# Attention scores: the rotary keys' high part times the queries' low part as 64-row matmuls, two key tiles side by side, four key tiles in one group

## The chip, the core and the metric

The kernel runs on one core of one Trainium2 chip. The metric is the time of one execution on the device in microseconds (us); the time before is the median of three runs, 1285.17 us (1284.21 to 1286.22).

The names of the engines: PE is TensorE (matmuls; PEld are its weight loads), DVE is VectorE, ACT is ScalarE, POOL is GpSimd, SP is SyncE, which issues most DMAs here.

## The reference

One layer of a bidirectional encoder, 2048 tokens of width 1024, all in float32. A combined projection feeds a gated linear attention (group A) and a latent attention with softmax (group B); their outputs pass one output projection, and a LayerNorm closes the layer. The change is in group B alone:

```python
def mla_branch(c_q, c_kv, k_rope, gate, positions, q_norm_g, w_uq, kv_norm_g, w_ukv):
    q = (rms_norm(c_q, q_norm_g) @ w_uq).reshape(B, S, MLA_HEADS, MLA_D_NOPE + MLA_D_ROPE)
    kv = (rms_norm(c_kv, kv_norm_g) @ w_ukv).reshape(B, S, MLA_HEADS, MLA_D_NOPE + MLA_DV)
    q_nope = q[..., :MLA_D_NOPE] * scale
    q_rope = apply_rope(q[..., MLA_D_NOPE:], positions) * scale
    k_nope, v = kv[..., :MLA_D_NOPE], kv[..., MLA_D_NOPE:]
    k_r = apply_rope(k_rope, positions)
    ...
        s = (jnp.einsum('bqhd,bkhd->bhqk', qn, k_nope, preferred_element_type=jnp.float32)
             + jnp.einsum('bqhr,bkr->bhqk', qr, k_r, preferred_element_type=jnp.float32))
        p = jax.nn.softmax(s, axis=-1)
        return jnp.einsum('bhqk,bkhv->bqhv', p.astype(v.dtype), v)
```

There are 4 heads; the plain part of a key has 128 numbers, the rotary part 64, and the rotary key is shared by all heads.

## The kernel before

**Precision.** A float32 operand that TensorE is to multiply is split into a high part (rounded to the type that TensorE takes in one pass, `F32R`) and a low part, the rest. A product of two such operands is made as three matmuls: high x high, high x low, low x high. `hi` makes a high part on ACT, `lo` a low part on DVE or POOL.

**Stages.** `sweep_a` (the linear attention's products), `late_gates`, `sweep_c` (the latent projections and the linear attention's end), then `attention`, whose tail is the output projection.

**Attention.** There are 16 blocks, one for each pair of a head and 512 queries. The key side is absorbed into the queries, so a block multiplies its queries with the 16 tiles of 128 latent keys that all heads share. A block goes through them in 8 steps j of two key tiles each. `scores(i, j)` fills one of two PSUM buffers `pS` (two banks each, one bank for each key tile e) with five matmuls of 128x512 for each key tile: latent keys' high part times the queries' high and low part, their low part times the high part, and two for the rotary part. For those the tile `kr` (profile name `krs`) holds a key's 64 rotary numbers twice over its 128 rows: high part on rows 0 to 63, low part on rows 64 to 127. The queries' parts `rh` and `rl` are fetched twice, on both halves of the rows; so `kr` x `rh` gives (high + low) x high in one matmul, and `kr` x `rl` gives (high + low) x low.

The other operations of a step, in the order of their dependencies:

- `copy(i, j)` on ACT (L1578) copies the scores from PSUM to SBUF; `smax(i, j)` on DVE (L1591, "max") takes the running maximum, reading the same PSUM buffer. The buffer is free for `scores(i, j+2)` after both.
- After step 7, `tmax`, `rmax` and `bmax` turn the maxima into one value for each query, on all rows.
- `sub` (DVE), `exp` (ACT, L1619), `phi` ("hi", ACT, L371, high part) and `plo` ("lo", POOL, L377, low part) make the softmax's numerators, and `pv(i, j)` multiplies them with the latent values: six matmuls (L425 to L427) that sum into `o`.
- `acc` and `tot` sum the numerators, `tsum` (four transposes on PE, L1678) and `rcp` make the reciprocal.
- After the last `pv`, `oh` (ACT, tile `ofh`) and `ol` (DVE, tile `ofl`) split `o`, `y` (three matmuls) multiplies it with the value weights, `yc` copies and stores.

**The order is written out by hand.** Each operation is put into a list with a place, counted in steps: `scores(i, j)` stands at 8i + j, an operation n of the same step at 8i + j + PLACE[n][j], and those that come once for each block at 8i + 7 + PLACE[n]. The list is sorted by place, and the operations are issued in that order; `in_order` ties each instruction to the one before it on its own engine, so every engine executes its part of the list in the order of the places and waits where an input isn't ready.

An operation of block i therefore runs while later blocks' scores are made. Around the change, in step 2 to 4 of block i, the places give these orders:

```
PE:  scores(i,2)  pv(i-2,6)  pv(i-2,7) at 2.45  scores(i,3)  tsum(i-2)  scores(i,4)  pv(i-1,0)
ACT: copy(i,2)  acc0  exp(i-1,1)  oh(i-2) at 3.34  hi(i-1,1) at 3.41  copy(i,3) at 3.73  hi(i-1,2)
DVE: max(i,2)  sub(i-1,4)  sub(i-1,5)  ol(i-2)  max(i,3)
```

Of the kernel before, what the change touches and what calls it, by code (L numbers as in the profile page):

```python
# [9 lines left out]
F32 = mybir.dt.float32  # L10
# [8 lines left out]
P = 128  # L19
# [10 lines left out]
QB = 512  # L30
# [51 lines left out]
    exp=(10.18, 9.95, 7.63, 9.15, 8.26, 9.12, 7.84, 8.01),  # L82
    hi=(10.39, 10.41, 9.81, 10.32, 9.82, 10.74, 10.53, 10.47),
    lo=(11.99, 11.22, 11.21, 12.62, 11.98, 11.51, 10.87, 10.63),
    pv=(12.35, 12.1, 11.89, 12.65, 12.27, 12.25, 12.14, 11.45),
    acc=(12.45, 11.78, 12.32, 0, 10.57, 11.24, 10.03, 9.22),
    acc0=10.78,
    tmax=1.26,
# [18 lines left out]
    pv=(16.29, 16.53, 21.45, 24.62, 26.22, 30.32, 41.89, 43.83),  # L107
# [17 lines left out]
    whole=(24.99, 55.73),  # L125
# [235 lines left out]
class K:  # L361
# [981 lines left out]

    def c_krsh(self, d):
        d["krs"] = self.w1.tile([P, 2, 64], F32R, tag="krs", name=f"krs{d['c']}")
        self.hi(d["krs"][:, 0], d["kr"][:, 0])

    def c_krsl(self, d):
        self.lo(d["krs"][:, 1], d["kr"][:, 0], d["krs"][:, 0], "pool")

    def c_vh(self, d):
        self.hi(self.vh[:, d["c"]], d["ckv"])
# [181 lines left out]
    def attention(self):  # L1534
        tc, nc = self.tc, self.nc
        mm = nc.tensor.matmul
        V, G, Ac = nc.vector, nc.gpsimd, nc.scalar
        NP = NKT // 2
        with ExitStack() as ctx:
# [5 lines left out]
            pM, pO, pX, pA, pS = bank("pM"), bank("pO"), bank("pX"), bank("pA"), bank("pS", 2)  # L1545
            blocks = [(h, b) for b in range(NQB) for h in range(H)]
            nb = len(blocks)
            stt = [dict(s=[None] * NP) for _ in blocks]

            def fetch(i):  # L1550
# [5 lines left out]
                for p, src in zip("hl", self.qr_s[b]):  # L1556
                    q.append(qp.tile([P, QB], F32R, tag="wz", name=f"r{p}{i}"))
                    for r in (slice(0, 64), slice(64, 128)):
                        nc.sync.dma_start(q[-1][r].bitcast(F32), src[h])

            def scores(i, j):


                d = stt[i]
                qh, ql, rh, rl = d["q"]
                ps = d["ps", j] = pS.tile([P, 2, QB], F32, tag="pS", name=f"pS{i}_{j}")
                for e in range(2):
                    kh, kl, kr = (t[:, 2 * j + e] for t in (self.ckvT_h, self.ckvT_l, self.kr))
                    mm(ps[:, e], kh, qh, start=True, stop=False)  # L1569
                    mm(ps[:, e], kh, ql, start=False, stop=False)  # L1570
                    mm(ps[:, e], kl, qh, start=False, stop=False)  # L1571
                    mm(ps[:, e], kr, rh, start=False, stop=False)  # L1572
                    mm(ps[:, e], kr, rl, start=False, stop=True)  # L1573

            def copy(i, j):
                d = stt[i]
# [166 lines left out]
            def put(place, fn, *a):  # L1743
                todo.append((place, len(todo), fn, a))

            def at(f, i, j=None):
                p = PLACE_LAST.get(f, PLACE[f]) if i == nb - 1 else PLACE[f]
                return p[j] if isinstance(p, tuple) else p
# [3 lines left out]
            for i in range(nb):  # L1752
                for j in range(NP):
                    t = NP * i + j
                    put(t, scores, i, j)
                    for n, f in (("copy", copy), ("max", smax), ("sub", sub), ("exp", exp), ("hi", phi), ("lo", plo),
                                 ("pv", pv), ("acc", acc)):
                        if n != "acc" or j != SUM_POOL[0] or i == nb - 1:
                            put(t + at(n, i, j), f, i, j)
                put(NP * i + at("acc0", i), acc0, i)  # L1760
                for n, f in (("tmax", tmax), ("rmax", rmax), ("bmax", bmax)) + {nb - 1: (), nb - 2: own_late}.get(i, own):
                    put(NP * i + NP - 1 + at(n, i), f, i)
                if i + 2 < nb:
                    put(NP * i + 4.05, fetch, i + 2)
# [298 lines left out]
```

## Time and profile before

| | |
|---|---|
| median of three runs | 1285.17 us (1284.21 to 1286.22) |
| the profiled execution's own time | 1286.1 us |
| its span, first to last instruction | 1284.3 us |
| mean granted TensorE clock | 0.998 |
| PE busy in the span | 98% |
| DVE, ACT, POOL busy in the span | 70%, 59%, 59% |

The attention's matmuls of scores run from 598 to 1079 us of the span. In the profile, a line such as `PE L1573 MATMUL pS<-rl,krs 128*128 128x512` is a matmul on 128 rows and 128 columns of the array with 512 columns streamed through it; "busy, mean ns" is its duration, which overlaps with the next matmul's. In a timeline the first number is the start and the second the duration (for "xN", from the first start to the last end), and in square brackets stands the idle time of the engine just before, with what ended it. In the table of windows each engine has its busy time and its number of instructions.

### The profile page before, as it was taken

How to read it: one execution, taken by the hardware profiler on the slowest of the kernel's cores; microseconds unless marked ns; L12 is line 12 of the kernel's file. 1: busy time of each engine (PE TensorE's matmuls, PEld its weight loads, DVE VectorE, ACT ScalarE, POOL GpSimd, SP SyncE). 2: the span in 40 equal slices, each digit the busy share in tenths (PEclk: the TensorE clock that was granted, in tenths of full speed). 3: DMA queues.
4: the chain of work that ended last, by engine and by line, in shares of the span. 5: the costliest groups of instructions: out<-in, count | busy, mean ns of one | idle time of the engine just before them, and what ended most of it. 6: DMA issues, size and time to landing. Idle time of an engine off the chain costs nothing.

```text
span 1284.3 us, 19837 instructions
## 1 busy us (share of the span) xinstructions
PE 1259.7 (98%) x7050; PEld 1109.9 (86%) x7050; DVE 899.4 (70%) x1602; ACT 755.5 (59%) x1230; POOL 761.1 (59%) x476
## 2 busy tenths in 40 slices
PE   7999999999999999999999999999999999999997
PEld 7999999999889999999788888888888888887886
DVE  6635554544575555554888888888888888479997
ACT  7544343444565655555788888888888888511110
POOL 0132323222367666650498888889999999944541
PEclk9999999999999999999999999999999999999999
DMA  8223444444755666547201111111133110375752
GB/s 293 78 79 108 115 111 114 115 105 126 255 171 184 205 205 210 194 149 228 76 1 42 41 42 50 46 54 58 58 89 93 41 42 9 123 227 193 220 189 99
DMA packets 135746, 155.25 MB, mean 121 GB/s; under 512 B 43510, under 2 KB 86142, under 8 KB 135648
## 3 DMA queue, kind: packets, MB, share of 16 engines
q1 hardware_dynamic: 127584, 151.86, 38.4%
q0 software_dynamic: 672, 2.10, 0.4%
q8 instruction: 56, 0.92, 0.4%
q10 hardware_dynamic: 7392, 0.03, 0.3%
q14 instruction: 42, 0.34, 0.2%
HBM read 100.43 MB, written 53.51 MB: 120 GB/s over the span
## 4 chain that ended last, share of the span: by engine, by line
PE 82%; DMA 5%; DVE 4%; ACT 2%; issue 2%; POOL 2%; SPq 2%; DVEq 0%; POOLq 0%; ACTq 0%
PE pz L1237 6%; PE ipm L1308 5%; PE o L425 4%; PE o L426 4%; PE o L427 4%; PE pS L1569 4%; PE pS L1570 4%; PE pS L1572 4%; PE pS L1571 4%; PE pS L1573 4%; PE ipa L425 4%; PE ipa L427 4%; PE ipa L426 4%; PE ipg L427 2%; PE ipg L425 2%
## 5 line engine op out<-in xcount | busy, mean ns | idle before, releaser
L377 POOL TENSOR_TENSOR pl<-s,ph 128x1024 fp32r<-128x1024 f32 x128 | 306.4, 2411 | 57.7 <-ACT ph L371 53.8
L1591 DVE TENSOR_TENSOR rm<-pS,rm 128x512 f32<-128x512 f32 x210 | 144.8, 689 | 36.7 <-ACT s L1578 31.5
L1578 ACT ACTIVATE s<-pS 128x1024 f32<-128x1024 f32 x128 | 131.2, 1026 | 61.8 <-PE pS L1573 52.0
L1615 DVE TENSOR_TENSOR s<-s,mb 128x1024 f32<-128x1024 f32 x128 | 151.2, 1212 | 8.9 <-PE mb L1609 8.2
L371 ACT ACTIVATE ph<-s 128x1024 fp32r<-128x1024 f32 x128 | 135.1, 1057 | 16.9 <-PE o L427 16.4
L1619 ACT ACTIVATE s<-s 128x1024 f32<-128x1024 f32 x128 | 131.4, 1050 | 12.2 <-DVE s L1615 12.1
L425 PE MATMUL ipa<-wah,xah 128*128 128x384 f32 (+1 forms) x384 | 129.7, 338 | 5.5 <-ACT wah L371 5.5
L426 PE MATMUL ipa<-wal,xah 128*128 128x384 f32 (+1 forms) x384 | 124.5, 324 | 0.5 <-DVE wal L377 0.5
L427 PE MATMUL ipa<-wah,xal 128*128 128x384 f32 (+1 forms) x384 | 124.4, 324 | 0.0
L1569 PE MATMUL pS<-qh,ckvT_h 128*128 128x512 f32 x256 | 102.7, 401 | 2.0 <-ACT s L1578 1.2
L1072 POOL TENSOR_TENSOR Sb<-Sb,Us 64x512 f32<-64x512 f32 x15 | 20.9, 1394 | 136.9 <-DVE Us L1064 127.8
L425 PE MATMUL o<-ph,vh 128*128 128x512 f32 x256 | 101.0, 395 | 0.0
L1570 PE MATMUL pS<-ql,ckvT_h 128*128 128x512 f32 x256 | 100.0, 391 | 0.0
L1572 PE MATMUL pS<-rh,krs 128*128 128x512 f32 x256 | 99.9, 390 | 0.0
L1571 PE MATMUL pS<-qh,ckvT_l 128*128 128x512 f32 x256 | 99.9, 390 | 0.0
L1573 PE MATMUL pS<-rl,krs 128*128 128x512 f32 x256 | 99.8, 390 | 0.0
L427 PE MATMUL o<-ph,vl 128*128 128x512 f32 x256 | 99.7, 389 | 0.0
L426 PE MATMUL o<-pl,vh 128*128 128x512 f32 x256 | 99.6, 389 | 0.0
L1642 DVE TENSOR_TENSOR ap<-ap,s 128x512 f32<-128x512 f32 x120 | 83.1, 693 | 2.7 <-ACT s L1619 0.7
L377 POOL TENSOR_TENSOR xal<-xaf,xah 128x1024 fp32r<-128x1024 f32 x12 | 29.7, 2477 | 87.8 <-ACT xah L371 87.8
L377 POOL TENSOR_TENSOR ol<-of,oh 128x512 fp32r<-128x512 f32 x32 | 43.2, 1352 | 62.6 <-ACT oh L371 61.9
L425 PEld LDWEIGHTS ipa<-wah,xah 128*128 128x128 f32 x384 | 72.9, 190 | 7.8 <-ACT wah L371 5.5
(308 smaller groups left out, 3595.6 us busy)
## 6 DMA issues: line engine op xcount, KB each, us to landing
xcf<-xT_dram SPq DMA_DIRECT2D x16, 512.0 KB, 5.1
xr<-x_dram SPq DMA_DIRECT2D x16, 512.0 KB, 6.4
out_dram<-rr SPq DMA_DIRECT2D x32, 256.0 KB, 2.2
xaf<-xT_dram SPq DMA_DIRECT2D x14, 512.0 KB, 4.2
oib<-oi_s SPq DMA_DIRECT2D x16, 256.0 KB, 4.0
qdb<-qd_s SPq DMA_DIRECT2D x16, 256.0 KB, 4.0
SU<-su_s SPq DMA_DIRECT2D x16, 256.0 KB, 4.1
ub<-u_s SPq DMA_DIRECT2D x16, 256.0 KB, 4.2
```

Source lines behind the costliest of these rows:

```text
L371: return nc.scalar.activation(dst, src, AF.Copy).ins
L377: return e.tensor_tensor(dst, src, hi.bitcast(F32), ALU.subtract).ins
L425: mm(out, ah, bh, start=start, stop=False)
L426: mm(out, ah, bl, start=False, stop=False)
L427: mm(out, al, bh, start=False, stop=stop)
L1569: mm(ps[:, e], kh, qh, start=True, stop=False)
L1570: mm(ps[:, e], kh, ql, start=False, stop=False)
L1571: mm(ps[:, e], kl, qh, start=False, stop=False)
L1572: mm(ps[:, e], kr, rh, start=False, stop=False)
L1573: mm(ps[:, e], kr, rl, start=False, stop=True)
L1591: V.tensor_tensor(d["rm"], src[:, e], d["rm"], ALU.max)
L1615: V.tensor_tensor(s, s, d["mb"][:, None, :].to_broadcast([P, 2, QB]), ALU.subtract)
```

## The change

The halves of `kr` are laid out the other way round for odd key tiles: low part on rows 0 to 63, high part on rows 64 to 127. So of two neighbouring key tiles the even one has its high part on the upper half of the rows and the odd one on the lower half.

In blocks 1 to 15, `scores` leaves out the matmul `kr` x `rl`. In its place a new operation `halves(i, j)`, for even j at place j + 0.22, makes only high part x `rl`, as matmuls of 64 rows: for the two key tiles of step j (one on rows 0 to 63, one on rows 64 to 127), and then for the two of step j + 1. The first two close the sums of step j; the last two open the buffer of step j + 1, to which `scores(i, j + 1)` then adds. The product of the keys' low part and the queries' low part is left out there. Block 0 keeps the five matmuls. `pv(i, 7)` gets another place, 12.3 instead of 11.45: in step 3 of block i + 2, behind `scores` and `tsum` and just ahead of `oh`.

```diff
-    pv=(12.35, 12.1, 11.89, 12.65, 12.27, 12.25, 12.14, 11.45),
+    pv=(12.35, 12.1, 11.89, 12.65, 12.27, 12.25, 12.14, 12.3),
...
     def c_krsh(self, d):
         d["krs"] = self.w1.tile([P, 2, 64], F32R, tag="krs", name=f"krs{d['c']}")
-        self.hi(d["krs"][:, 0], d["kr"][:, 0])
+        self.hi(d["krs"][:, d["j"]], d["kr"][:, 0])
 
     def c_krsl(self, d):
-        self.lo(d["krs"][:, 1], d["kr"][:, 0], d["krs"][:, 0], "pool")
+        j = d["j"]
+        self.lo(d["krs"][:, 1 - j], d["kr"][:, 0], d["krs"][:, j], "pool")
...
+            def bank_pair(i, j):
+                if ("ps", j) not in stt[i]:
+                    stt[i]["ps", j] = pS.tile([P, 2, QB], F32, tag="pS", name=f"pS{i}_{j}")
+                return stt[i]["ps", j]
+
             def scores(i, j):
-                d = stt[i]
-                qh, ql, rh, rl = d["q"]
-                ps = d["ps", j] = pS.tile([P, 2, QB], F32, tag="pS", name=f"pS{i}_{j}")
+                qh, ql, rh, rl = stt[i]["q"]
+                begun = i > 0 and j % 2
+                whole = i == 0
+                ps = bank_pair(i, j)
                 for e in range(2):
                     kh, kl, kr = (t[:, 2 * j + e] for t in (self.ckvT_h, self.ckvT_l, self.kr))
-                    mm(ps[:, e], kh, qh, start=True, stop=False)
+                    mm(ps[:, e], kh, qh, start=not begun, stop=False)
                     mm(ps[:, e], kh, ql, start=False, stop=False)
                     mm(ps[:, e], kl, qh, start=False, stop=False)
-                    mm(ps[:, e], kr, rh, start=False, stop=False)
-                    mm(ps[:, e], kr, rl, start=False, stop=True)
+                    mm(ps[:, e], kr, rh, start=False, stop=bool(begun))
+                    if whole:
+                        mm(ps[:, e], kr, rl, start=False, stop=True)
+
+            def halves(i, j):
+
+                rl = stt[i]["q"][3]
+                for n in (j, j + 1):
+                    ps = bank_pair(i, n)
+                    for e in range(2):
+                        r = slice(64 * e, 64 * e + 64)
+                        mm(ps[:, e], self.kr[r, 2 * n + e], rl[r], start=n > j, stop=n == j)
...
                     put(t, scores, i, j)
+                    if i and j % 2 == 0:
+                        put(t + 0.22, halves, i, j)
```

## The prediction

> **What bounds the kernel now.** I read the page first: engine shares, then the group of the product that is changed.
>
> ```profile
> span 1284.3 us, 19837 instructions
> PE 1259.7 (98%) x7050; PEld 1109.9 (86%) x7050; DVE 899.4 (70%) x1602; ACT 755.5 (59%) x1230; POOL 761.1 (59%) x476
> L1573 PE MATMUL pS<-rl,krs 128*128 128x512 f32 x256 | 99.8, 390 | 0.0
> ```
>
> PE is busy for 98% of the span, and the product kr x rl is 256 of its 7050 matmuls. Since a share is an average over stages, the next view is the busy time of each engine in the attention's steady part.
>
> ```profile
> 645.00:1049.00 404.00, 404.00 (x1857) 334.31 (x1857) 351.06 (x469) 333.85 (x359) 360.21 (x156) 1.00 0.19 50
> ```
>
> The columns are window, length, then PE, weight loads, DVE, ACT, POOL, then clock and DMA. In 404 us PE never pauses, and the clock is full. DVE, ACT and POOL stand at 87, 83 and 89%: not the bound, but little slack, so when they run decides whether PE must wait. The timeline of one block (i = 6), first PE, then ACT, then DVE:
>
> ```profile
> 782.32 0.39 PE L427 MATMUL o<-ph,vl 128*128 128x512 f32 x1
> 782.54 0.39 PE L1569 MATMUL pS<-qh,ckvT_h 128*128 128x512 f32 x1
> ...
> 784.58 0.39 PE L1573 MATMUL pS<-rl,krs 128*128 128x512 f32 x1
> 784.82 0.60 PE L1678 MATMUL sx<-ident,acc 128*128 128x128 f32 x4
> 785.17 0.48 PE L1569 MATMUL pS<-qh,ckvT_h 128*128 128x512 f32 x1
> 785.48 0.40 PE L1570 MATMUL pS<-ql,ckvT_h 128*128 128x512 f32 x1
> ```
>
> ```profile
> 782.74 0.60 ACT L371 ACTIVATE ofh<-o 128x512 fp32r<-128x512 f32 x1 [0.17 <-PE o L427]
> 783.24 1.05 ACT L371 ACTIVATE ph<-s 128x1024 fp32r<-128x1024 f32 x1
> 785.07 1.03 ACT L1578 ACTIVATE s<-pS 128x1024 f32<-128x1024 f32 x1 [0.79 <-PE pS L1573]
> 786.00 1.05 ACT L371 ACTIVATE ph<-s 128x1024 fp32r<-128x1024 f32 x1
> 786.94 2.00 ACT L1619 ACTIVATE s<-s 128x1024 f32<-128x1024 f32 x2
> ```
>
> ```profile
> 778.90 1.40 DVE L1591 TENSOR_TENSOR rm<-pS,rm 128x512 f32<-128x512 f32 x2
> 784.93 0.68 DVE L377 TENSOR_TENSOR ofl<-o,ofh 128x512 fp32r<-128x512 f32 x1
> 786.13 1.42 DVE L1591 TENSOR_TENSOR rm<-pS,rm 128x512 f32<-128x512 f32 x2 [0.52 <-ACT s L1578]
> 792.83 1.42 DVE L1591 TENSOR_TENSOR rm<-pS,rm 128x512 f32<-128x512 f32 x2
> 799.77 1.42 DVE L1591 TENSOR_TENSOR rm<-pS,rm 128x512 f32<-128x512 f32 x2 [0.85 <-ACT s L1578]
> ```
>
> Durations of matmuls overlap, so a slot is read from starts: ten slots from 782.54 to 784.82 make 0.227 us each. The four transposes take 785.17 - 784.82 = 0.35, and the slot behind them is 0.08 longer (785.17 to 785.48). Read ACT with the places of the code: oh(i-2) starts 0.20 after pv(i-2, 7) has given up its slot (782.54), then hi(i-1, 1), and only then copy(i, 3), which here waits for PE. ACT executes in this order, always.
>
> **The change, part by part.** *The product.* In blocks 1 to 15 the sixteen full matmuls with rl become sixteen 64-row ones, in four groups of two pairs: 60 groups, in each 4 slots = 0.907 us out, and two pairs in. The count of matmuls stays 7050. What does a group cost? The trace holds a model, the product Ap in the first stage: eight pairs on rows 0-63 and 64-127, each half into another PSUM bank, between full matmuls.
>
> ```profile
> 324.79 0.34 PE L426 MATMUL ipa<-wal,xah 128*128 128x384 f32 x1
> 324.96 0.33 PE L427 MATMUL ipa<-wah,xal 128*128 128x384 f32 x1
> 325.23 1.16 PE L1035 MATMUL Ap<-qd,kd 64*128 64x128 f32 x16
> 326.32 0.44 PE L425 MATMUL ipa<-wah,xah 128*128 128x384 f32 x1
> 326.60 0.34 PE L426 MATMUL ipa<-wal,xah 128*128 128x384 f32 x1
> ```
>
> Narrow windows on the end of that group show two pairs, then the last one:
>
> ```profile
> 326.00 0.39 PE L1035 MATMUL Ap<-qd,kd 64*128 64x128 f32 x4
> 326.11 0.28 PE L1035 MATMUL Ap<-qd,kd 64*128 64x128 f32 x2
> ```
>
> The two of the last pair together take 0.28, one alone 0.27: they run side by side. Pairs follow each other at 0.11. Now the price of going in and out. A slot of 384 columns is 0.17 (324.79 to 324.96), so without the group L426 would have started at 324.96 + 2 x 0.17 = 325.31; it starts at 326.60. The group took 1.29, its eight pairs account for 8 x 0.11 = 0.89, and 0.40 is left: about 0.1 of waiting and 0.1 of a weight load that nothing hides, on the way in (324.96 + 0.17 = 325.13, start at 325.23) and again on the way out (326.11 + 0.11 = 326.22, start at 326.32; the next start 0.28 later instead of 0.17). [...]
>
> So a group costs 2 x 0.227 + 0.40 = 0.854 and saves 0.05: 60 x 0.05 = 3 us. The bounds: a switch at 0.2 (weight loads hidden in 512 columns) saves 15 us, one at 0.55 loses 6. I take 0.40, since the nearest row has it.
>
> *krs halves swapped for odd key tiles, rl fetched as before.* The same instructions with other columns: nothing. Leaving out the low part of kr costs nothing either.
>
> *The bank taken early.* The second pair of halves(i, j) opens the buffer of scores(i, j+1). There are two buffers, so copy(i, j-1) and max(i, j-1) must be over when PE is only behind scores(i, j). Each of the four places, with u = 0.227 and the second pair 8u + 0.2 + u = 2.24 behind the start of scores(i, j):
>
> ```profile
> 773.81 0.48 PE L1569 MATMUL pS<-qh,ckvT_h 128*128 128x512 f32 x1
> ...
> 793.92 0.39 PE L1569 MATMUL pS<-qh,ckvT_h 128*128 128x512 f32 x1
> ...
> 800.49 0.39 PE L1569 MATMUL pS<-qh,ckvT_h 128*128 128x512 f32 x1
> ```
>
> These start scores 1, 6, and 0 of the next block. For j = 0: scores0 at 800.49, pair due at 802.73, max7 over at 799.77 + 1.42 = 801.19: free. For j = 6: due at 793.92 + 2.24 = 796.16, max5 over at 794.25: free. For j = 2: from scores1 at 773.81 come 8u, pv5 (6u), scores2 (8u), pv6 (6u), then 0.43: 28u + 0.43 + 0.08 = 6.87 later, 780.68, and max1 is over at 780.30: free by 0.4, the tightest. The price if that cover fails is the difference, 0.3 a block.
>
> For j = 4 it isn't free, because pv(i-2, 7) is moved too, from ahead of scores3 to between scores3 and scores4. oh needs the finished sum of pv7, and oh still stands ahead of hi1 and copy3 on ACT. Take the end of pv7's slot as 0:
> - oh starts at 0.20, hi1 at 0.70 (782.74 to 783.24), copy3 0.94 behind hi1's start (786.00 to 786.94 for such a pair): 1.64. Copy start to the end of max3 is 786.13 + 1.42 - 785.07 = 2.48: 4.12.
> - PE at that time has scores4 (8u = 1.81), the way in 0.20 and the first pair 0.23: it stands at 2.24.
>
> PE waits 4.12 - 2.24 = 1.88. Waking costs something too; block 1 shows it, where scores3 waits for max1 (DVE, then PE):
>
> ```profile
> 625.71 1.41 DVE L1591 TENSOR_TENSOR rm<-pS,rm 128x512 f32<-128x512 f32 x2
> ```
>
> ```profile
> 627.26 0.47 PE L1569 MATMUL pS<-qh,ckvT_h 128*128 128x512 f32 x1 [0.42 <-DVE rm L1591]
> 627.57 0.40 PE L1570 MATMUL pS<-ql,ckvT_h 128*128 128x512 f32 x1
> ```
>
> The max ends at 627.12, PE starts 0.14 later, and its first slot is 0.31 instead of 0.23. With 0.14 + 0.08 the wait is 2.1 us per block. Behind the waiting pair PE has pv(i-1, 0) and scores5; copy5 waits for the latter, copy4 doesn't, since the first pair closed its bank. Nothing gives the time back: DVE, ACT and POOL get 2 us of slack per block, which buys nothing where PE is the bound. ol on DVE (784.93) now waits for oh, but max3 behind it waits for copy3 longer. Only blocks 2 to 15 have a pv7 two blocks back: 14 waits.
>
> In block 1 nothing stands between scores3 and scores4, and max3 ends late:
>
> ```profile
> 632.21 1.41 DVE L1591 TENSOR_TENSOR rm<-pS,rm 128x512 f32<-128x512 f32 x2
> ```
>
> ```profile
> 632.56 0.39 PE L425 MATMUL o<-ph,vh 128*128 128x512 f32 x1
> ```
>
> pv0 then starts at 633.62 + 0.22 + 0.23 + 0.2 = 634.27 instead of 632.56, 1.7 late; 0.5 of it comes back in the second half of the block (six slots fewer, 0.85 for a group), so 1.2, at most 1.7 if the pair at j = 0 waits as well. I take 1.5.
>
> *Sum.* Each of 14 blocks: 2.1 lost, 4 x 0.05 saved, 1.9; 14 x 1.9 + 1.5 = 28 us. The profiled execution took 1286.1 us (span 1284.3), 0.9 above the median 1285.17: 1314.
>
> **The rivals.** *The wait isn't there (not slower).* If copy3 got onto ACT before oh, max3 would be over 787.55 - 784.82 = 2.73 behind scores3, while the second pair comes 0.35 + 0.08 + 6u + 2.24 = 4.03 behind it: no wait in the 14 blocks, and 1286.1 + 1.5 - 14 x 0.2 = 1285, the same as now. The mechanism is pv7 used as cover for copy3 and max3; it decides where the wait falls below 0.2 per block. Against it: ACT's order in the rows above, with oh right behind pv7's end.
>
> [...]
>
> *The halves run one after the other.* With 512 columns they might not share the array: 60 x 2u = 27 us more, 1341. Against: the pair of 326.11.
>
> **How the numbers follow.** The forecast's mechanism gets 0.80, no wait 0.08, a free switch 0.06, serial halves 0.06. Within the forecast, a wait of 1.7 to 2.4 makes 1308 to 1318, switches of 0.2 to 0.55 make 1302 to 1323, and a short wait at j = 2 adds up to 4. With the free switch's 1290 at the low end the range is 1289 to 1326, and 0.14 lies outside. A measurement of this kernel tells 0.2% (2.6 us) from no change. Faster: half of the no-wait case and the free switch without a wait, 0.06; same: the rest of the no-wait case and a sliver of the free switch, 0.06; slower: 0.88.
>
> **What would show it.** Right: a new PE line with 240 matmuls of 64*128 on krs and rl, L1573's successor with 16; PE idle before that line, released by DVE's max (or PE's weight loads so), about 30 us in 14 to 15 waits; on ACT, oh waiting for PE and copy3 starting at once behind hi1, no longer released by PE; a block period of 33 us instead of 31.1; in each group about 0.1 lost on both sides. Wrong: no idle time on PE in step 4 (then the no-wait rival), a first full matmul right behind the pair (free switch), or starts of a pair 0.2 apart (serial).

## The result, and the profile after

The changed kernel takes 1328.04 us (median of four runs, 1327.2 to 1329.05) against 1285.49 before: ratio 1.0333, 95% interval 1.0316 to 1.0349. It is 42.5 us slower; 28 were forecast, and the time lies 2 us above the range. The page of the changed kernel, then its granted clock:

```profile
span 1326.4 us, 19797 instructions
PE 1276.1 (96%) x7050; PEld 1090.5 (82%) x7050; DVE 897.6 (68%) x1602; ACT 756.2 (57%) x1230; POOL 762.6 (57%) x476
L1589 PE MATMUL pS<-rl,krs 64*128 64x512 f32 x240 | 49.3, 464 | 27.7 <-DVE rm L1607 27.7
```

```profile
core 0: 1326.4 us, clock 0.987
```

The 240 half matmuls are there, and 27.7 us of PE's idle time stand ahead of them, ended by max on DVE. From block 2 on these are 14 waits (in all, times, longest):

```profile
PE pS L1589 <- DVE rm L1607: 25.7, 14, 1.9
```

What was not forecast is the clock: 0.987 instead of 0.998. One block (i = 6) of the changed kernel, PE, then ACT, then DVE; here `copy` is L1594 and `max` L1607:

```profile
800.74 0.39 PE L1578 MATMUL pS<-rh,krs 128*128 128x512 f32 x1
801.06 0.50 PE L1589 MATMUL pS<-rl,krs 64*128 64x512 f32 x2
803.39 0.49 PE L1589 MATMUL pS<-rl,krs 64*128 64x512 f32 x2 [1.83 <-DVE rm L1607]
803.82 0.50 PE L425 MATMUL o<-ph,vh 128*128 128x512 f32 x1
```

```profile
799.33 0.60 ACT L371 ACTIVATE ofh<-o 128x512 fp32r<-128x512 f32 x1 [1.55 <-PE o L427]
799.83 1.05 ACT L371 ACTIVATE ph<-s 128x1024 fp32r<-128x1024 f32 x1
800.78 1.01 ACT L1594 ACTIVATE s<-pS 128x1024 f32<-128x1024 f32 x1
```

```profile
799.97 0.69 DVE L377 TENSOR_TENSOR ofl<-o,ofh 128x512 fp32r<-128x512 f32 x1
801.83 1.42 DVE L1607 TENSOR_TENSOR rm<-pS,rm 128x512 f32<-128x512 f32 x2 [1.17 <-ACT s L1594]
```

This is the forecast chain: oh waits 1.55 for pv7, then hi1, then copy3 with no wait of its own, then max3 until 803.25, and 0.14 later the second pair. It starts 2.33 behind the first; without a wait a second pair follows 0.33 behind the first (785.24 to 785.58 in this block's first group), so the wait costs 2.0. (The profile's 1.83 counts from the end that it gives the first pair, 801.06 + 0.50; its slot is over 0.16 earlier. Below, idle times within a window count from the slot's end; the waits of the experiments are the profile's.) A group that doesn't wait, between full matmuls:

```profile
794.37 0.39 PE L427 MATMUL o<-ph,vl 128*128 128x512 f32 x1
794.69 0.73 PE L1589 MATMUL pS<-rl,krs 64*128 64x512 f32 x4
795.35 0.50 PE L1575 MATMUL pS<-qh,ckvT_h 128*128 128x512 f32 x1
795.69 0.39 PE L1576 MATMUL pS<-ql,ckvT_h 128*128 128x512 f32 x1
```

Without the group L1576 would start two slots behind 794.37, at 794.82; it starts 0.87 later. Four full slots are 0.907, so a group saves 0.04.

Now the clock. Windows of 3.41 us, PE alone (length, PE busy, clock, DMA):

```profile
731.31:734.72 3.41, 1.58 (x8) 1.00 0.00 0
734.72:738.13 3.41, 3.41 (x9) 0.50 0.09 5
799.57:802.98 3.41, 1.99 (x9) 1.00 0.00 0
802.98:806.40 3.42, 3.01 (x13) 1.00 0.08 3
```

In one block the whole wait, 732.07 to 734.06, lies in one such window, and the next window has half the clock; call such a window a half window. In another the wait (801.40 to 803.39) is cut by the edge at 802.98, and the clock stays full. The profiled execution has nine half windows in the attention, and their starts lie a whole number of 3.413 us apart. Of the 14 waits nine lie inside one window, and these nine are followed by a half window; the other five are cut, 1.6 on one side and 0.4 on the other, and none is. (The changed kernel's other three executions had a clock of 0.986 to 0.988, so about as many.) The starts of the transposes mx (of the maxima) of successive blocks, 31.1 apart before, are now 33.1 apart without and 34.6 with a half window. So the account of the attention is 14 x 1.95 = 27 us for the waits with what the groups save, 9 x 1.57 = 14 for the half windows, 1.5 in block 1: 43, of which the end of the attention gives 1 back. The span grew by 42.1.

### The profile page after: what moved, and what is told of

It reads as the page before. It is cut to its first block, busy times and chain, and to the rows that moved or that the text cites. A ratio compares the mean times of both kernels' runs of the same rounds, so it can differ in the third digit from the quotient of the medians.

```text
span 1326.4 us, 19797 instructions
## 1 busy us (share of the span) xinstructions
PE 1276.1 (96%) x7050; PEld 1090.5 (82%) x7050; DVE 897.6 (68%) x1602; ACT 756.2 (57%) x1230; POOL 762.6 (57%) x476
## 4 chain that ended last, share of the span: by engine, by line
PE 79%; DVE 5%; DMA 5%; ACT 5%; issue 2%; POOL 2%; SPq 2%; DVEq 0%; POOLq 0%; ACTq 0%
PE pz L1237 6%; PE o L425 5%; PE ipm L1308 5%; PE o L427 5%; PE o L426 5%; PE pS L1575 4%; PE ipa L425 4%; PE pS L1576 4%; PE ipa L427 4%; PE ipa L426 4%; PE pS L1577 4%; PE pS L1578 4%; PE pS L1589 3%; PE po L427 2%; PE po L425 2%
## 5 line engine op out<-in xcount | busy, mean ns | idle before, releaser
L1607 DVE TENSOR_TENSOR rm<-pS,rm 128x512 f32<-128x512 f32 x210 | 145.0, 690 | 72.3 <-ACT s L1594 68.1
L1594 ACT ACTIVATE s<-pS 128x1024 f32<-128x1024 f32 x128 | 130.9, 1023 | 68.8 <-PE pS L1589 38.2
L425 PE MATMUL o<-ph,vh 128*128 128x512 f32 x256 | 108.3, 423 | 0.0
L1575 PE MATMUL pS<-qh,ckvT_h 128*128 128x512 f32 x256 | 106.0, 414 | 1.4 <-ACT s L1594 1.1
L427 PE MATMUL o<-ph,vl 128*128 128x512 f32 x256 | 104.3, 407 | 0.0
L426 PE MATMUL o<-pl,vh 128*128 128x512 f32 x256 | 104.0, 406 | 0.0
L1576 PE MATMUL pS<-ql,ckvT_h 128*128 128x512 f32 x256 | 101.0, 395 | 0.0
L1589 PE MATMUL pS<-rl,krs 64*128 64x512 f32 x240 | 49.3, 464 | 27.7 <-DVE rm L1607 27.7
```

Source lines behind the costliest of these rows:

```text
L425: mm(out, ah, bh, start=start, stop=False)
L426: mm(out, ah, bl, start=False, stop=False)
L427: mm(out, al, bh, start=False, stop=stop)
L1575: mm(ps[:, e], kh, qh, start=not begun, stop=False)
L1607: V.tensor_tensor(d["rm"], src[:, e], d["rm"], ALU.max)
```

## The experiments

Each kernel is the changed one with the edit shown, unless it says otherwise; "before" is run on the same chip.

**oh_ol_late: the wait taken away**

```diff
-    oh=12.34,
-    ol=12.99,
+    oh=12.75,
+    ol=13.25,
```

> The changed kernel with oh (ACT) and ol (DVE) at later places, 12.75 and 13.25, so that copy(i,3) and max(i,3) run before them. Theory: the 42 us are 14 waits of 1.95 us of the second pair at j = 4 (27 us), some 1.5 us in block 1, and 14 us in which the clock stands at half after such waits. With the waits gone the clock stays full, the groups save 4 x 0.04 us per block: 1284 to 1286 us, PE idle before the halves under 2 us, mean clock 0.998. Rival (the 64-row matmuls or their switches lower the clock, not the waits): clock 0.987 stays, 1298 to 1300 us.

Measured: 1288.23 us, ratio 1.0022 (1.0013 to 1.0031), clock 0.999, no half window. The 64-row matmuls alone don't lower the clock, and 40 of the 42.5 us hung on what oh held up. It is 2 us more than expected: each block still loses 0.12 instead of gaining 0.17. At j = 4 the second pair follows 0.43 behind the first instead of 0.33, and pv0 0.50 behind it instead of 0.32, since it opens `o`, which ol, now behind max3, reads late.

**pv_back: the moved pv put back**

```diff
-    pv=(12.35, 12.1, 11.89, 12.65, 12.27, 12.25, 12.14, 12.3),
+    pv=(12.35, 12.1, 11.89, 12.65, 12.27, 12.25, 12.14, 11.45),
```

> The changed kernel with pv(i,7) back at 11.45, ahead of scores3. Theory: oh no longer holds copy3; the second pair at j = 4 is due 2.67 us behind the end of scores3's slots and max3 is over 2.73 behind it, plus 0.14 to wake: waits of 0.2 to 0.3 us in each block, no half clock, 1287 to 1290 us. Rival (the moved pv is not the cause, the bank taken early is): waits near 2 us stay, above 1315 us.

Measured: 1295.91 us, ratio 1.0084 (1.007 to 1.0098), clock 0.999. Between the two expectations. The waits on PE, then ACT and DVE in one block:

```profile
PE pS L1589 <- ACT s L1635: 7.5, 14, 0.5
```

```profile
785.01 1.03 ACT L1594 ACTIVATE s<-pS 128x1024 f32<-128x1024 f32 x1 [1.53 <-PE pS L1589]
...
788.82 1.03 ACT L1594 ACTIVATE s<-pS 128x1024 f32<-128x1024 f32 x1
```

```profile
789.66 0.68 DVE L377 TENSOR_TENSOR ofl<-o,ofh 128x512 fp32r<-128x512 f32 x1
790.26 1.40 DVE L1607 TENSOR_TENSOR rm<-pS,rm 128x512 f32<-128x512 f32 x2
```

The wait at j = 4 is 0.54 and ends with max3 at 791.66 (the line names exp on ACT, which ended last near it). I had kept copy3 and max3 at their distance from before. But the bank of step 2 is now closed by halves(i, 2), behind pv6, so copy2 waits 1.53 for PE, and acc0, exp, oh and hi1 are late behind it; ol then stands ahead of max3. So the move of pv7 isn't the only cause: without it there are 11 us left.

**move_only: the kernel before with pv7 moved, and nothing else**

```diff
-    pv=(12.35, 12.1, 11.89, 12.65, 12.27, 12.25, 12.14, 11.45),
+    pv=(12.35, 12.1, 11.89, 12.65, 12.27, 12.25, 12.14, 12.3),
```

> The kernel before with only pv(i,7) moved to 12.3. Theory: copy3 and max3 run late here too, but no one takes the bank before scores5, some 5 us later; no wait, 1285 to 1286 us. Rival (the move alone makes PE wait): 1300 us or more.

Measured: 1297.39 us, ratio 1.0096 (1.0082 to 1.011), clock 0.998. The expectation was wrong:

```profile
PE pS L1569 <- DVE rm L1591: 6.2, 14, 0.4
```

scores5 opens the bank that max3 reads. Behind pv7 come ten slots of scores4 and six of pv0, 3.7 us, not the 5 that I wrote; the chain oh, hi1, copy3, max3 takes 4.12 + 0.14. This wait is not the whole loss of 12.4: by its starts a block takes 0.9 longer, of which 0.68 is lost at scores5 (it starts 0.60 late, and its first slot is 0.08 longer) and 0.15 in the same way at scores6. That the order needs pv7 ahead of scores3 could have been seen before.

**full_rows: the early bank and the moved pv, without 64-row matmuls**

```diff
-                        r = slice(64 * e, 64 * e + 64)
-                        mm(ps[:, e], self.kr[r, 2 * n + e], rl[r], start=n > j, stop=n == j)
+                        mm(ps[:, e], self.kr[:, 2 * n + e], rl, start=n > j, stop=n == j)
```

> The changed kernel with halves made as full matmuls of 128 rows (kr x rl, as in the kernel before), at the same places and into the same banks: the bank taken early and the moved pv without 64-row matmuls. Theory: the waits and the half clock stay, only the 0.04 us per group is lost: 1328 to 1333 us, mean clock 0.987. Rival (64-row matmuls cause the drop of the clock): clock 0.998, 1314 to 1318 us.

Measured: 1327.5 us (1323.46 to 1328.31), ratio 1.0331 (1.0315 to 1.0347), 0.5 below the expected range. The same time as the changed kernel, with ordinary matmuls; the waits are the same:

```profile
PE pS L1588 <- DVE rm L1606: 25.3, 14, 1.8
```

The profiled execution, the fastest of the four, had a span of 1321.7 and five half windows, clock 0.992; the others had a clock of 0.988 to 0.989, nearer to the 0.987 expected. So the clock falls without 64-row matmuls too.

**own_pair: 64-row pairs without the early bank**

```diff
-                begun = i > 0 and j % 2
+                begun = False
...
-                for n in (j, j + 1):
+                for n in (j,):
...
-                    if i and j % 2 == 0:
-                        put(t + 0.22, halves, i, j)
+                    if i:
+                        put(t, halves, i, j)
```

with pv(i, 7) at 11.45.

> 64-row pairs without the bank taken early: each scores(i,j) in blocks 1 to 15 closes with its own pair, 120 groups of one pair instead of 60 of two, and pv(i,7) at 11.45. Theory: no wait, no half clock; a group of one pair costs 0.227 + 0.41 us in place of two slots (0.453): 120 x 0.18 = 22 us, 1306 to 1309 us. Rival (the switch is free in 512 columns): 120 x 0.227 saved, 1258 us. Rival (64-row matmuls lower the clock): above 1320 us.

Measured: 1305.89 us, ratio 1.0162 (1.0148 to 1.0176), clock 0.999: 21 us for 120 groups, 0.17 each, where 0.18 was expected. This measures the price of going in and out by itself: 0.17 + 0.453 - 0.227 = 0.40. With a free switch this kernel would be 120 x 0.227 = 27 us faster, and the measurement decides against that for groups as short as these. How much of the 0.40 is waiting, and how much the loading of weights, the runs don't show.

**hi_first and hi2_first: a shorter and a longer wait**

```diff
-    oh=12.34,
+    oh=12.42,
```

> The changed kernel with oh at 12.42, behind hi(i-1,1) on ACT: the high part is then made while ACT waits for pv7, and the chain oh, copy3, max3 is 0.95 us shorter. Theory: PE's idle time at j = 4 is 0.9 instead of 1.83 us in each of 14 blocks, which is too short to halve the clock: 14 x 1.0 + 1.5 us, 1298 to 1303 us, clock 0.999. Rival (any wait there halves the clock in most blocks): 1310 us or more, clock under 0.99.

```diff
-    hi=(10.39, 10.41, 9.81, 10.32, 9.82, 10.74, 10.53, 10.47),
+    hi=(10.39, 10.41, 9.72, 10.32, 9.82, 10.74, 10.53, 10.47),
```

> The changed kernel with hi(i-1,2) ahead of copy(i,3) on ACT (place 9.72 instead of 9.81): 0.95 us more between pv7 and copy3. Theory: idle time of 2.8 us in each of 14 blocks, of which a fixed window of 3.41 us holds enough to halve the clock in nearly every block: 14 x 2.9 + 1.5 and 10 to 14 half windows of 1.6 us, 1342 to 1351 us, clock 0.98. Rival (the half windows come from something else, 9 as before): 1341 us.

Measured: 1301.13 us, ratio 1.0125 (1.0109 to 1.014), for the first; 1341.48 us, ratio 1.0433 (1.0414 to 1.0452), for the second. Waits on PE of the first and of the second:

```profile
PE pS L1589 <- DVE rm L1607: 12.5, 14, 0.9
```

```profile
PE pS L1589 <- DVE rm L1607: 39.0, 14, 2.8
```

Waits of 0.9 gave no half window (clock 0.999). The second kernel was expected to have 10 to 14 and had six in its profiled execution (span 1335.0), in four of its 14 blocks. Its block of 34.05 us is nearly ten windows of 3.413, so the place of the wait in the windows moves by 0.1 us only from block to block, and most waits stay cut:

```profile
698.37:701.78 3.41, 2.11 (x10) 1.00 0.01 2
701.78:705.19 3.41, 1.92 (x8) 1.00 0.02 5
705.19:708.61 3.42, 3.42 (x16) 1.00 0.07 1
906.58:909.99 3.41, 0.75 (x4) 1.00 0.01 3
909.99:913.40 3.41, 3.28 (x8) 0.50 0.10 5
```

The first wait is cut into 1.46 and 1.49, and the clock stays; the second leaves 2.83 in one window, and the next one is half. Two other waits were cut into 1.91 and 1.0: there the window behind the first piece is half, and so is the one after it. In this execution 1.86 or less in a window at full clock was followed by none.

This is one execution of four. The other three took 1340.69 to 1342.81, with a clock of 0.985 to 0.987; worked out from their clocks and spans, they had some nine or ten half windows (an estimate). So the median lies just under the range, and the time alone can't be told from the rival's 1341; what speaks for the fixed windows is where the half windows stand in the trace.

Nor do the runs give a sharp limit: in full_rows five of ten windows with 1.95 to 1.97 were followed by a half window, and five were not. What decides there stays open.

**filled: the same wait, with PE kept busy**

```diff
                 ps = bank_pair(i, j)
+                for _ in range(8 if i > 1 and j == 4 else 0):
+                    mm(ps[:, 0], self.ckvT_h[:, 8], qh, start=True, stop=True)
```

> The changed kernel with eight idle matmuls of 128x512 ahead of scores(i,4) in blocks 2 to 15, into the bank that scores(i,4) then opens anew: 112 matmuls whose results are thrown away, 1.81 us of PE work in each block in the place of the wait. Theory: the wait's 27 us stay (max3 sets when the second pair can run), but PE is no longer idle there, so the clock stays full and the 14 us of half clock go: 1312 to 1316 us, clock 0.999. Rival (the 14 us come from the switches, or the longer path is set by PE's work): 1328 us with the clock at 0.987, or 1350 us and more (112 x 0.227 = 25 us added).

Measured: 1314.55 us, ratio 1.0229 (1.0213 to 1.0245). The stage's window of the changed kernel (length, PE, weight loads, DVE, ACT, POOL, clock, DMA), then this kernel's clock and the same window of it:

```profile
645.00:1085.00 440.00, 416.12 (x1842) 315.29 (x1841) 350.02 (x466) 330.60 (x356) 355.70 (x155) 0.97 0.17 46
```

```profile
core 0: 1313.2 us, clock 0.999
```

```profile
645.00:1085.00 440.00, 439.66 (x2013) 335.92 (x2012) 360.24 (x478) 341.04 (x369) 368.40 (x160) 1.00 0.18 48
```

112 matmuls that nobody reads make the kernel 13.5 us faster (1328.04 to 1314.55). That separates the two terms: 29 us of waiting for max3, with block 1, and 14 us of half clock, which are gone where PE is busy for 439.66 of the 440.00 us.

**best and three_groups: can the halves win?** The first takes oh_ol_late, leaves block 1 as block 0, and puts sub(i-1, 5) behind max3:

```diff
-    sub=(9.47, 8.65, 7.39, 7.37, 7.49, 6.63, 6.95, 7.44),
+    sub=(9.47, 8.65, 7.39, 7.37, 7.49, 7.24, 6.95, 7.44),
...
-    oh=12.34,
-    ol=12.99,
+    oh=12.75,
+    ol=13.22,
...
-                begun = i > 0 and j % 2
-                whole = i == 0
+                begun = i > 1 and j % 2
+                whole = i < 2
...
-                    if i and j % 2 == 0:
+                    if i > 1 and j % 2 == 0:
```

> The version with the later oh and ol, mended where its trace still waits: block 1 keeps the five matmuls (its two waits cost 1.5 us), and sub(i-1,5) stands behind max(i,3) on DVE (place 7.24 instead of 6.63, ol at 13.22). Theory: of the 0.12 us that each of 14 blocks still lost, 0.1 of waiting at the second pair goes, 0.1 to 0.2 at pv0 stays, the groups save 4 x 0.04: 1284 to 1286 us, the same as the kernel before within 0.1%. Rival (the halves can win once all waits are gone): 1282 us or less.

Measured: 1292.86 us, ratio 1.0061 (1.0049 to 1.0074), worse than oh_ol_late. A new wait took the place of the old:

```profile
PE pS L1575 <- DVE rm L1607: 2.8, 14, 0.2
```

It stands ahead of scores6, which opens the bank that max4 reads; sub5, put behind max3, pushes max4. By the starts, scores6 and its first slot lose 0.45 in each block, more than the four groups of 0.04 save, and pv0 still starts 0.16 late. The second keeps halves where no wait followed:

```diff
-                begun = i > 0 and j % 2
-                whole = i == 0
+                begun = i > 1 and j in (1, 3, 7)
+                whole = i < 2 or j in (4, 5)
...
-                    if i and j % 2 == 0:
+                    if i > 1 and j in (0, 2, 6):
```

with pv(i, 7) at 11.45.

> Groups of halves only where no wait follows: j = 0, 2 and 6 of blocks 2 to 15; steps 4 and 5 and blocks 0 and 1 keep the five matmuls, pv(i,7) is back at 11.45. Theory: scores4 opens its own buffer late enough for max2, scores5 for max3; 14 x 3 groups save 0.04 us each, 1.8 us in all: 1282.5 to 1285 us. Rival (other waits of the tight DVE and ACT chain come up, as in the version before): 1287 us or more.

Measured: 1284.0 us against 1285.17, ratio 0.9989 (0.998 to 0.9997), clock 0.998, and no wait of PE from block 2 on. The gain expected, 42 groups of 0.04, is 1.7 us; the medians are 1.2 us apart, and the interval of the ratio stands for 0.4 to 2.6 us. So the idea is worth about 1 us here.

## Why the prediction was wrong

*Right, by its own steps.* The sign; the switch (0.40 forecast, 0.40 in own_pair, a group 0.87 instead of 0.854); the free places j = 0, 2 and 6; the wait at j = 4, its chain over oh, hi1, copy3 and max3, and its price (2.1 forecast, 2.0 measured); block 1 (1.5 and 1.5); serial halves (the two of a pair start 0.003 us apart) and a free switch (0.40 in own_pair), both excluded. The 24 us, 60 x 0.40, behind the free switch's 1290 no run shows: own_pair measured that price, 0.40 for each group. A kernel that has just these terms, filled, takes 1314.55, where 1314 was forecast.

*The step that failed* is the price of the wait in the sum: "2.1 lost" in each of 14 blocks counts the wait's length and nothing else. The clock was read off a window in which PE never paused ("the clock is full") and put at nothing for a kernel in which PE does pause, without a reason given. A wait has a second price here: 2.0 us of idle PE inside one window of 3.41 us cost the next window half its clock, 1.57 us of time, in nine of 14 blocks. The sum lacked this term of 14 us, and the range held only the spread of the terms that it had.

*The rival without a wait* was forecast at 1285 for copy3 ahead of oh; that kernel, oh_ol_late, took 1288.23, since the second pair and pv0 then start a little late. And the cover has a price that was not seen: the move costs 12 us by itself (move_only), and without it the halves still cost 11 (pv_back). Each delays copy3, the move through oh, the early bank in pv_back through copy2. In the changed kernel the way through copy2 doesn't count, since ACT stands idle for 1.55 us ahead of oh until pv7 is over. The 2 us that reach the clock there are the chain behind the moved pv7, met by a bank that is wanted ahead of pv0; in move_only the same chain meets scores5, behind pv0, and leaves 0.4.

## What to carry to other kernels

A wait put into a dense stream of matmuls can be priced twice: its length, and what the clock does after it. Here 2.0 us inside one window had both prices, waits of 0.9 us (hi_first) the first alone. Before an operation is moved in a fixed order, follow what stands behind its consumer on the consumer's engine: here one place on PE moved oh, and with it copy3 and max3, past the moment when PE wanted the bank. And a packed group of matmuls has to save more than its two ends cost: 0.40 us, against 0.45 saved by two pairs of 512 columns.

## What the runs showed of the hardware

- In the changed kernel's attention the clock stood at 0.50 in nine windows of 3.413 us, whose starts lie a whole number of 3.413 us apart. There 2.0 us of idle PE inside one window was followed by half the clock in the next (nine of nine); the same idle time cut by an edge into 1.6 and 0.4 was not (none of five), and waits of 0.9 us by the profile were not (hi_first). Between these there is no sharp limit: 1.91 was followed by half windows twice in hi2_first, 1.95 to 1.97 in five of ten cases in full_rows.
- A longer wait did not cost more clock: with waits of 2.8 us by the profile, one execution of hi2_first (clock 0.990) had half windows in four of 14 blocks, against nine in the changed kernel (0.987) with waits of 1.8 by the profile; ten of the waits were cut by an edge into pieces of 1.86 or less. In the other three executions the clock was as low as with the shorter waits (0.985 to 0.987, against 0.986 to 0.988).
- Two 64-row matmuls of 512 columns on the two halves of the rows, into two banks, start 0.003 us apart and run side by side (0.49 us for one, 0.50 for both); changing between 64 and 128 rows cost 0.40 us for in and out (own_pair, 120 groups).
